# The first tile of a decoder block: x loaded first, its modulation shared by VectorE and TensorE, four weight buffers, and attention's casts queued behind the last hT

## The chip, the cores and the metric

The kernel runs on one core of a Trainium2 chip. The metric is the device time of one execution in microseconds; the time quoted for a kernel is the median of its runs. Engines are called PE (TensorE, with PEld for its weight loads), DVE (VectorE), ACT (ScalarE), POOL (GpSimd) and SP (SyncE, which issues most of the DMAs).

## The reference, cut to what matters

One decoder layer over 512 positions of width 1024, all in float32. The change touches its first stage only: the modulated RMSNorm and the first 768 columns of the input projection.

```python
cs = jax.nn.silu(c)
mod = cs @ w_ada[l] + b_ada[l]
shift1, scale1, gate1, shift2, scale2, gate2 = [m[:, None, :] for m in jnp.split(mod, 6, axis=-1)]
h = _rmsnorm(x, norm1_g[l]) * (1.0 + scale1) + shift1
proj = h @ w_in[l]
qa, ka, va, qd, kd, vd, ga, gd = jnp.split(proj, points, axis=-1)
# sliding-window attention (qa, ka, va), differential attention (qd, kd, vd), gates (ga, gd),
# merge and output projection, then a second modulated RMSNorm, an MLP with a causal convolution, a last RMSNorm
```

shift1 and scale1 are matrix-vector products: each needs 1024 x 1024 weights of w_ada, 4 MB, and they scale and shift h per column.

## The kernel before, in words

Width 1024 is cut into eight tiles of 128 columns (KT = 8), the positions into four tiles of 128 rows (NT = 4). The first stage produces, for each of the eight tiles k, hT(k): 128 columns of h transposed, 128 x 512, as a high part hTh (in fp32r, a rounded float32) and a low part hTl (the rest). A projection tile is then three products: high weights by hTh, low weights by hTh, high weights by hTl. mm_k(k, part) issues one of these for the six banks acc6, which are 768 columns of qa, ka, va: six matmuls of 128 x 128 by 128 x 512 (L334), 18 per tile k. They add up in the same six banks over all eight tiles, so attention can start only after tile 7.

What tile k needs:

- **x**: four transfers of 512 KB into xn (L214). stat(t) squares and sums on ACT (L351), rstd_start does ms on DVE (L171) and a power on POOL (L175), rstd_end finishes on DVE (L181, L185). normalise(t) scales the first HEAD = 256 columns on DVE (L358); scale_x scales the rest on ACT (L381). turn(t) (L363) transposes tile 0, h_turn(k) (L315) the others.
- **The modulation of its 128 columns**: adaw(k), two transfers of 512 KB (scale and shift columns of w_ada; L207) into two buffers. ac_ops forms the sum of the eight weight rows times cs (silu of c) on DVE: two scalings (L256), six multiply-adds (L258), one add (L260), each over 256 columns. reduce_mod sums the 128 partitions on PE with a column of ones (pa, L267), and finish_mod adds bias and gain on DVE (mod, L276, L279). PE issues each float32 matmul as two instructions.
- **hT**: h_tile (L320) writes hTh and hf on ACT from the transposed x with scale and bias from mod; h_low (L324) forms hTl on DVE.
- **Its weights**: w0(k), 384 KB into four raw buffers (L220); split_hi casts them on ACT (L299, L300), split_lo forms the low parts on DVE (L306, L308).

SP issues the transfers in the written order: crow8 (c itself), adaw0, x, w0_0, adaw1, w0_1, and so on. Within a manual schedule DVE, ACT and PE issue in the written order; POOL is outside of it here, and the framework's scheduler placed POOL's constants (qsc, dsw, ddf) and the clearing of va (L436) at the start. keep_warm issues small matmuls into a bank that is not in use yet (L341): 14 at the start, and three behind each of the first three turns.

The loop over the tiles puts the next tile's preparation among the present tile's matmuls: DVE does ac_ops for tile k+1, with h_low(k) in between; PE does the next turn, parts 0 and 1, then the sums pa for tile k+1, then part 2.

Behind the stage comes attention. fill(n) issues n steps of units: a load of eight 128 x 128 weight blocks (L477), a cast on ACT and a low part on DVE (split_pair, L115, L116), and the matmuls (pq, pk, pw; L119 to L121). Each step has three matmuls of 512 columns. evac_q and evac move the six banks out (L430 to L434, L445). ACT and DVE are placed by the scheduler there.

## Time and profile before

| what | value |
|---|---|
| median of 3 runs | 715.82 us (714.96 to 717.16) |
| the profiled execution, its own time | 716.59 us |
| its span, first to last instruction | 714.5 us |
| instructions | 11275 |
| DVE, ACT, POOL busy | 588.5, 384.2, 84.4 us |
| moved by DMA | 121.82 MB, 170 GB/s on the mean |
| DMA, 0 to 20 us and 20 to 62 us | 310 and 254 GB/s |
| first projection matmul of tiles 0, 1, 7 | 19.40, 24.87, 56.44 us |
| first matmul of attention's units (pq) | 60.72 us |

A row of the timeline gives the start and the duration in us, the engine, the line in the kernel, the operation, output and inputs by the program's names, the shapes and a count of merged instructions; in brackets stands the idle time of that engine before it and what ended it. A row of the windows view gives a stretch, its length, the busy time of PE, PEld, DVE, ACT and POOL with the instructions in brackets, the granted TensorE clock as a share of full speed, the mean busy share of the DMA engines and the rate. Times in the trace are from the start of the span. The profiled execution is one of the program's executions; its time differs from the median.

### The profile page before, as it was taken

The page shows a single profiled execution, that of the slowest core. Times are in us where ns is not written, and L with a number is a line of the kernel's source. Part 1 is how long each engine was busy: PE and PEld are TensorE (multiplying, and loading weights), DVE is VectorE, ACT ScalarE, POOL GpSimd, SP SyncE. Part 2 cuts the span into 40 slices and gives each one's busy share as a digit, 9 for nine tenths or more (in the row PEclk, how much of TensorE's full clock was granted, in tenths as well). Part 3 has the DMA queues.
Part 4 walks back from the last instruction along what each step waited for, and adds up shares of the span by engine and source line. Part 5 has one row for each costly group of instructions (what it writes and reads, how often), then busy time and mean ns, then how long its engine had stood idle before and what let it go on. Part 6 is the DMA issues. An engine that isn't in the chain of part 4 may idle for free. (4 is left out here: it accounts for less than half of the span.)

```text
span 714.5 us, 11275 instructions
## 1 busy us (share of the span) xinstructions
PE 688.4 (96%) x4187; PEld 603.0 (84%) x4187; DVE 588.5 (82%) x1125; ACT 384.2 (54%) x677; POOL 84.4 (12%) x101
## 2 busy tenths in 40 slices
PE   5999899999999999999999999999999999999994
PEld 5777778777787888888879999999999999888884
DVE  5998978797986774865479899888889899979996
ACT  3646566455554233432258666555555666656664
POOL 4000000001000100000012021111111102540300
PEclk9999999999999999999999999999999999999998
DMA  9983522453553664737717598877789738996903
GB/s 307 293 264 96 173 64 83 148 163 102 151 159 105 225 196 140 235 118 210 232 59 148 153 201 203 191 185 217 190 199 229 164 123 233 182 203 194 160 0 119
DMA packets 115863, 121.82 MB, mean 170 GB/s; under 512 B 4415, under 2 KB 93280, under 8 KB 115808
## 3 DMA queue, kind: packets, MB, share of 16 engines
q1 hardware_dynamic: 96894, 95.09, 42.1%
q0 software_dynamic: 18720, 25.73, 21.2%
q8 instruction: 33, 0.54, 0.3%
q10 hardware_dynamic: 194, 0.28, 0.1%
q14 instruction: 22, 0.18, 0.1%
HBM read 118.97 MB, written 2.11 MB: 169 GB/s over the span
## 5 line engine op out<-in xcount | busy, mean ns | idle before, releaser
L1133 PE MATMUL up<-t,m_whi 128*128 128x256 f32 x528 | 96.1, 283 | 0.0
L1133 PEld LDWEIGHTS up<-t,m_whi 128*128 128x128 f32 x528 | 82.3, 192 | 0.0
L1133 PE MATMUL up<-t,m_wlo 128*128 128x256 f32 x264 | 74.7, 283 | 0.1
L1133 PE MATMUL up<-bh,p_wlo 128*128 128x256 f32 x232 | 65.7, 284 | 0.6 <-DVE p_wlo L1076 0.6
L1133 PE MATMUL up<-bh,p_whi 128*128 128x256 f32 x232 | 65.6, 283 | 0.0
L1133 PE MATMUL up<-bl,p_whi 128*128 128x256 f32 x232 | 65.6, 283 | 0.0
L1133 PEld LDWEIGHTS up<-t,m_wlo 128*128 128x128 f32 x264 | 50.6, 192 | 0.3 <-DVE m_wlo L1076 0.3
L1133 PEld LDWEIGHTS up<-bh,p_wlo 128*128 128x128 f32 x232 | 44.4, 192 | 1.1 <-DVE p_wlo L1076 1.1
L1133 PEld LDWEIGHTS up<-bh,p_whi 128*128 128x128 f32 x232 | 44.5, 192 | 0.0
L1133 PEld LDWEIGHTS up<-bl,p_whi 128*128 128x128 f32 x232 | 44.5, 192 | 0.0
L1044 POOL DMA_DIRECT2D s<-in_w_up_dram x21 | 27.2, 1385 | 143.0 <-DMA s<-in_w_up_dram 92.7
L764 DVE SCALAR_TENSOR_TENSOR arow<-ra,cs,arow 128x512 f32<-128x512 f32 x56 | 41.9, 748 | 1.4 <-DMA ra<-in_w_ada_dram 0.7
L1076 DVE TENSOR_TENSOR m_wlo<-s,m_whi 128x1024 fp32r<-128x1024 f32 x31 | 37.7, 1216 | 2.0 <-ACT m_whi L1072 2.0
L1072 ACT CAST m_whi<-s 128x1024 fp32r<-128x1024 f32 x31 | 32.5, 1047 | 9.3 <-DVE s L1066 5.9
L1133 PE MATMUL up<-t,p_whi 128*128 128x256 f32 x176 | 32.2, 283 | 0.0
L175 POOL TENSOR_TENSOR r<-ms,mhalf 128x1 f32<-128x1 f32 (+1 forms) x16 | 13.4, 838 | 144.7 <-DVE ms L173 77.2
L694 ACT ACTIVATE sd<-sd,dmx 128x128 f32<-128x128 f32 (+3 forms) x32 | 17.8, 556 | 22.0 <-DVE dmx L692 15.4
L777 POOL DMA_DIRECT2D mod_rows<-arow x8 | 4.3, 540 | 200.5 <-ACT arow L776 200.3
L1133 PEld LDWEIGHTS up<-t,p_whi 128*128 128x128 f32 x176 | 27.4, 192 | 0.2 <-issue 0.2
L1140 ACT ACTIVATE gT<-a,cv 128x512 f32<-128x512 f32 x22 | 17.7, 813 | 17.6 <-DVE a L1175 17.3
L1072 ACT CAST p_whi<-wa 128x1024 fp32r<-128x1024 f32 x18 | 18.7, 1042 | 12.0 <-PE up L1133 10.8
L1133 PE MATMUL up<-t,p_wlo 128*128 128x256 f32 x88 | 24.9, 283 | 0.0
(485 smaller groups left out, 2119.5 us busy)
## 6 DMA issues: line engine op xcount, KB each, us to landing
ra<-in_w_ada_dram SPq DMA_DIRECT2D x32, 512.0 KB, 4.2
wa<-in_w_up_dram SPq DMA_DIRECT2D x22, 512.0 KB, 4.6
s<-in_w_up_dram SPq DMA_DIRECT2D x21, 512.0 KB, 5.0
s<-in_w_up_dram POOLq DMA_DIRECT2D x21, 512.0 KB, 6.5
adaw<-in_w_ada_dram SPq DMA_DIRECT2D x16, 512.0 KB, 5.1
w<-in_w_in_dram SPq DMA_DIRECT2D x12, 512.0 KB, 3.9
a<-in_w_up_dram SPq DMA_DIRECT2D x11, 512.0 KB, 4.7
b<-in_w_down_dram SPq DMA_DIRECT2D x10, 512.0 KB, 3.9
```

The costliest lines, as they stand in the source:

```text
L175: nc.gpsimd.tensor_tensor(r0, ms, mhalf[:, :n], ALU.pow)
L694: nc.scalar.activation(pm[m], pm[m], AF.Exp, bias=mx[:, m : m + 1], scale=slope, accum_out=lsum[:, m : m + 1])
L764: nc.vector.scalar_tensor_tensor(ac, r[:, a], cc, ac, ALU.mult, ALU.add)
L777: nc.gpsimd.dma_start(mod_rows[idx : idx + 1, hf * S : (hf + 1) * S], row)
L1044: nc.gpsimd.dma_start(dst, upblock(*blk), accum_op=ALU.add)
L1072: nc.scalar.copy(W[J, name][0], R[J, SRC[name]])
L1076: nc.vector.tensor_sub(lo, R[J, SRC[name]], hi.bitcast(F32))
L1133: nc.tensor.matmul(o[u], w[:, k, cu], b[:, k], start=name in ("p1", "m5", "p2") and k == 0 and x == 0, stop=k == 3 and x == 2, skip_group_ ...
L1140: nc.scalar.activation(grow(j), av[J][:, u], AF.Identity, bias=cv[:, 66 + j : 67 + j], scale=cv[:, 44 + j : 45 + j])
```

## The change

- SP issues x first; crow8 goes to ACT's queue. adaw0 follows in five parts, the scale columns ahead of the shift columns, then w0_0 in two. adaw has four buffers; tiles 1 and 2 load their adaw in four parts.
- Tile 0's modulation: DVE sums three of the eight weight rows (own_rows, once for scale and once for shift, over 128 columns), PE multiplies the other five by cs directly (mod_mm, with the weights stationary and 48 equal columns of cs moving) and adds DVE's sum (own_sum). For tile 1 PE takes three of the eight rows (direct); tiles 2 to 7 leave all eight to DVE. The sums for tiles 1 to 7 have 48 columns in place of one.
- Bias and gain of mod go to ACT (finish_one); hT(0) and the casts of w0_0 are shared by ACT and DVE; tile 0's matmuls take the banks in the order 4, 5, 0, 1, 2, 3.
- normalise(t) and turn(t) follow stat(t) directly; the keep-warm matmuls are 4, 11, 4 and 5. h_turn(1) comes ahead of tile 0's matmuls.
- POOL joins the manual schedule, and its constants and the clearing of va are written behind the loop.
- Attention's first casts on ACT are ordered behind hf(7), by issue_after, which orders the issue of instructions of the same engine only.

```diff
-    nc.sync.dma_start(crow8, c.rearrange("o (a p) -> (o a) p", p=P))
+    nc.scalar.dma_start(crow8, c.rearrange("o (a p) -> (o a) p", p=P))
...
-        aw = pp.tile([P, 2, KT, m * P], F32, tag="adaw", bufs=2, name=f"adaw{k}")
...
-    load_ada(groups[0])
     for t in range(NT):
-        nc.sync.dma_start(xn[:, t], xd[t * P : (t + 1) * P, :])
...
+        load_x(t)
+    for lo in (0, 4):
+        load_ada_part(adaw[0], 0, 0, 1, lo, lo + 4)
+    for lo, hi in ((0, 4), (4, 6), (6, 8)):
+        load_ada_part(adaw[0], 1, 0, 1, lo, hi)
+    load_w0(0, (512, 768))
+    load_w0(0, (0, 512))
+    for g in groups[1:]:
+        load_ada(g, (0, 4, 8) if g[0] < 3 else (0, 8))
+        load_w0(g[0])
...
-    man.enter_context(tc.manual_schedule(engines={nc.vector.engine, nc.scalar.engine, nc.tensor.engine}))
+    man.enter_context(tc.manual_schedule(engines={nc.vector.engine, nc.scalar.engine, nc.tensor.engine, nc.gpsimd.engine}))
+    keep_warm(4)
...
+    def direct(gi):
+        return {1: 3}.get(gi, 0)
+    NB = 48
+    def mod_mm(o, aw, j, lo, hi, start, stop=True):
         for kk in range(lo, hi):
+            nc.tensor.matmul(
+                o, aw[:, j, kk], cs[:, kk : kk + 1].to_broadcast([P, NB]),
+                start=start and kk == lo, stop=stop and kk == KT - 1,
             )
+    def reduce_one(o, gi, j):
+        more = direct(gi)
+        mod_mm(o, adaw[gi], j, KT - more, KT, True, False)
+        nc.tensor.matmul(o, ac[gi][0][:, j], ones[:, 0:NB], start=not more, stop=True)
+    def finish_one(k, o, j):
...
+        if j == 0:
+            nc.scalar.activation(m[:, 0:1], o[:, 0:1], AF.Identity, bias=cb[:, k : k + 1], scale=n1g[:, k : k + 1])
+        else:
+            nc.scalar.activation(m[:, 1:2], o[:, 0:1], AF.Identity, bias=bsh[:, k : k + 1])
...
+    OWN = 3
+    def own_rows(j):
+        for kk in range(OWN):
+            if kk == 0:
+                nc.vector.tensor_scalar_mul(a0[:, j], adaw[0][:, j, kk], cs[:, kk : kk + 1])
+            else:
+                nc.vector.scalar_tensor_tensor(a0[:, j], adaw[0][:, j, kk], cs[:, kk : kk + 1], a0[:, j], ALU.mult, ALU.add)
+    def own_sum(j):
+        nc.tensor.matmul(po[j], a0[:, j], ones[:, 0:NB], start=False, stop=True)
+    keep_warm(11)
...
+    stat(0)
+    normalise(0)
+    turn(0)
+    keep_warm(4)
+    stat(1)
...
+    normalise(1)
+    turn(1)
+    keep_warm(5)
+    stat(2)
+    normalise(2)
+    turn(2)
+    stat(3)
+    own_rows(0)
+    mod_mm(po[0], adaw[0], 0, OWN, 8, True, False)
+    own_sum(0)
+    scale_x(0)
+    scale_x(1)
+    normalise(3)
+    mod_mm(po[1], adaw[0], 1, OWN, 4, True, False)
+    turn(3)
+    own_rows(1)
+    mod_mm(po[1], adaw[0], 1, 4, 8, False, False)
+    own_sum(1)
...
+    nc.scalar.copy(wts[0][0][:, 512:768], w0[0][:, 512:768])
+    finish_one(0, po[0], 0)
+    nc.vector.tensor_copy(wq, rq)
+    nc.vector.tensor_add(m[:, 1:2], po[1][:, 0:1], bsh[:, 0:1])
+    nc.scalar.activation(hTh[0][:, :256], pts[0][:, :256], AF.Identity, bias=m[:, 1:2], scale=m[:, 0:1])
+    nc.vector.tensor_scalar(hTh[0][:, 256:], pts[0][:, 256:], m[:, 0:1], m[:, 1:2], ALU.mult, ALU.add)
+    nc.scalar.activation(hfs[0], pts[0], AF.Identity, bias=m[:, 1:2], scale=m[:, 0:1])
+    split_lo(0, 1)
     split_lo(0, 0)
+    scale_x(2)
+    scale_x(3)
+    h_turn(1)
...
-            ac_ops(gi + 1, 0, AC_CUT)
+            ac_ops(gi + 1, 0, AC_CUT if gi else 2)
         h_low(g[0])
         if nxt:
-            ac_ops(gi + 1, AC_CUT, KT)
+            ac_ops(gi + 1, AC_CUT if gi else 2, KT)
...
+    # behind the loop now: qsc, dsw and ddf on POOL, unchanged
+    va = big.tile([P, 2, 4, 2 * P], F32R, tag="kvB", name="va")
+    nc.gpsimd.memset(va.bitcast(F32), 0.0)
...
-    fill(SWA_FILL[0])
+    with tc.issue_after(tiles[KT - 1].ins):
+        fill(SWA_FILL[0])
```

## The prediction

> **What bounds the kernel now.** I read the page first. Its first part has PE busy for 688.4 of 714.5 us, and the second part puts the thin places at the two ends and near 366 us.

> ```profile
> PE 688.4 (96%) x4187; PEld 603.0 (84%) x4187; DVE 588.5 (82%) x1125; ACT 384.2 (54%) x677; POOL 84.4 (12%) x101
> ...
> PE   5999899999999999999999999999999999999994
> ```

> Of the 26 us in which PE does nothing, 8.9 lie before 20 us (by the windows view PE is busy for 11.11 of the first 20), and much of that busy time is keep-warm work. From 20 to 366 us PE stands for about 6. So whatever brings tile 0's first projection matmul forward should move everything behind it, as long as no other engine takes over. The PE timeline shows that start: start, duration, engine, line, operation, count, and in brackets the idle time before with its releaser.

> ```profile
> 12.62 0.33 PE L363 MATMUL xt<-ident,xn 128*128 128x128 f32 x1 [2.75 <-DVE xn L358]
> 12.79 0.83 PE L341 MATMUL a<-ones,ident 128*128 128x128 f32 x6
> ...
> 16.87 1.49 PE L341 MATMUL a<-ones,ident 128*128 128x128 f32 x6
> 18.15 0.38 PE L363 MATMUL xt<-ident,xn 128*128 128x128 f32 x1
> 18.36 0.61 PE L315 MATMUL xt<-ident,xn 128*128 128x128 f32 x4
> 19.40 1.66 PE L334 MATMUL a<-hThA,w0h 128*128 128x512 f32 x6 [0.43 <-ACT hThA L320]
> ```

> The first projection matmul starts at 19.40. Its chain backwards: ACT's hT(0), x's last transpose, a keep-warm burst queued in front of that transpose, x normalised by DVE (16.44 to 16.79), its statistics on ACT from 13.05, and x itself, which comes behind 1.05 MB of adaw0:

> ```profile
> 9.24 1.06 ACT L351 ACTIVATE sq<-xn 128x1024 f32<-128x1024 f32 x1 [6.39 <-DMA xn<-in_x_dram]
> ```

> Then the windows view, cut at the first matmul of tiles 0, 1, 2, 3 (the columns are PE, PEld, DVE, ACT, POOL, the granted clock, the DMA share and GB/s).

> ```profile
> 19.40:24.87 5.47, 5.31 (x26) 4.25 (x26) 4.94 (x15) 5.47 (x9) 0.00 (x0) 1.00 0.79 263
> 24.87:29.95 5.08, 5.08 (x26) 4.25 (x27) 4.73 (x14) 2.71 (x5) 0.00 (x0) 1.00 1.02 327
> 29.95:35.27 5.32, 5.27 (x30) 4.14 (x28) 5.13 (x15) 2.25 (x5) 0.00 (x0) 1.00 0.87 272
> ```

> A tile takes 5.08 us where PE is alone in deciding (tile 1) and 5.3 to 5.4 in tiles 2 to 5, where DVE is busy for 5.13 to 5.26: DVE finishes ac late, PE's pa matmuls wait (PE starts them 0.2 us after its sixth matmul could have ended), and DVE then waits 0.16 for pa. Last, two rows that price a clash:

> ```profile
> 5.33 1.18 DVE L243 TENSOR_SCALAR cols<-cols 128x8 f32<-128x8 f32 x1
> ...
> 4.69 1.80 POOL L436 MEMSET va<- 128x2048 f32 x1
> ```

> An instruction of the size of L171's (0.15 us) ends at 6.51, right after POOL's memset (6.49). L235 does the same behind POOL's iota (2.91 to 3.46): it ends at 3.48.

> **Step 1, x first.** Today x0 lands 6.97 us after its issue at 2.27. adaw0's 1.05 MB, 3.0 us at the 341 to 366 GB/s of 4 to 7 us, are no longer ahead, and SP starts with x at 0.74 instead of crow8 (0.45 us). So x0 lands at 9.24 - 3.45 = 5.8 at the latest. The other end: adaw0's 1.05 MB were in use 5.55 us after their issue; half of it is 1.5 less, so 0.74 + 4.05 = 4.8. I take 5.25. Three more x tiles, 1.57 MB at 0.40 MB/us (8 to 12 us: 393 to 418 GB/s), are in at 9.1. adaw0 and w0_0, 1.44 MB at 0.35, follow until 13.2; w0_0 in today's order (issued 5.03, 8.9 to landing) gives 13.9 - 0.45 = 13.5. Splitting adaw0 into five issues of 0.37 to 0.5 us keeps SP at under 6 us of issues, so issue is not the limit. crow8 now heads ACT's queue and delays the rows by 0.4 us; their reader (cols) has until 9 us.

> **Step 2, normalisation.** Per x tile: ACT 1.25 (1.06 + 0.19), then DVE ms 0.15, POOL pow 0.65, DVE rt, rst and xn 0.8. In DVE's new order each tile's three steps stand behind the one before, so tiles follow at 1.65. First: 5.25 + 1.25 + 1.65 = 8.15; then 9.8, 11.45; the fourth waits besides for own_rows(0), three instructions on 128 columns (0.75, between nothing and the 1.35 that three on 256 columns take): x is normalised at 13.1. Today: 16.79.

> **Step 3, modulation of tile 0.** Eight whole-width ac instructions and an add on DVE become six half-width ones; the rest is 10 matmuls with 48 columns, two PE instructions each. Nearest rows: 128 columns at full clock, six in 0.67 us (12.79 to 13.46), 0.11 each; one column, 0.09 each. After turn(3) (13.3) eight instructions of shift rows take 0.9, own_sum and its drain 0.4, the add on DVE 0.15. hT(0) is halved between ACT and DVE (0.78 for the whole, so 0.45 to 0.5). First matmul: 15.4, against 19.40: **-4.0**. If PE runs at half clock the 18 mod and sum instructions cost 0.22 each (the burst at 16.87), 1.0 to 1.6 more on this path; with the early ends of x and own_rows it is 14.4.

> **Step 4, tile 0 itself** (5.47 today). PE: parts 0 and 1 take 2.9, six direct matmuls for tile 1's mod 1.3 (12 at 0.11), the sums 0.4, part 2 1.48, the next turn 0.35: 6.45. DVE after hT(0) (15.2): split_lo 1.0, two ac scalings 0.55, h_low 0.6, three ac steps 1.25, the add 0.4: 19.0, just when PE gets there (15.4 + 2.9 + 0.65). But POOL is now in the written order, so the constants stand behind the fourth pow (12.25): eight memsets 1.1 us, iota and selects 2.1, va's memset 1.8, in all until 17.25. DVE's scalings fall at about 16.15, within the memset, and wait 1.1 as L243 did. PE waits the same in front of its first ac sum. Tile 0 takes 7.55: **+2.1**; without the clash +1.0. The ends are +0.7 (no clash, and 0.09 for each small matmul) and +2.8 (the memset is met at its start).

> **Step 5, tiles 1 to 6** (31.57 from tile 1's first matmul to tile 7's). The mod's two DVE instructions (0.20 from start to start) go to ACT, which is busy for only 2.3 of 5.3 us, and DVE stops waiting for pa (0.16): about 4.95 on DVE, under PE's 5.08. 48 columns for one add at most 0.08. So 5.10 five times and 4.78 for tile 6 (5.07 less its wait of 0.27): 30.28, **-1.3**, between -0.3 and -1.6. ACT's two small instructions (0.2 each) fit into the 0.4 us that hT is early today. Four adaw buffers let SP run ahead (it waits 8.9 us for DVE at L207 today): adaw2 lands at 20.8, needed at 21; from then 1.44 MB per tile take 4.1 to 4.3 us.

> **Step 6, entry to attention.** Casts of the first two weights (L115, 1.04 each) now stand behind hf(7) on ACT: they end 2.6 us after tile 7's first matmul, DVE's low parts (1.21 each) at 2.75 and 4.0, and PE asks at 4.3. So nothing, hidden by tile 7's matmuls; if the five evacuations (4.0 us of ACT) came first, up to 4.2. Only ACT is held: loads stay as they are.

> Sum: -4.0 + 2.1 - 1.3 = **-3.2**. The profiled execution took 716.59 (span 714.5), so 713.4; it lay 0.8 above the median of 715.82, so **712.6**.

> **Rivals.** (a) No clash: the scalings miss POOL's memset. For it: adaw1 may come late enough to push them behind 17.25. Then -4.3: 711.5. (a') The clash comes earlier too: POOL's iota and selects (0.34 to 0.61 each, 13.35 to 15.45) meet own_rows(1) and the copy of w0_0 on DVE (13.1 to 14.6), and one select's wait of 0.6 with a part of a second one puts the first matmul 0.8 later: 713.4. For it: L235 behind the iota; against: only single-input DVE instructions are seen waiting, and the trace has none with two SBUF inputs beside a select. [...] (b) Half clock in tile 0. The windows view has it today after a stretch in which PE was thinly used:

> ```profile
> 12.00:15.00 3.00, 1.34 (x11) 1.26 (x11) 1.44 (x9) 2.85 (x6) 1.18 (x2) 0.99 1.16 351
> 15.00:18.35 3.35, 3.24 (x15) 3.24 (x16) 3.13 (x13) 0.01 (x1) 0.79 (x2) 0.50 1.06 335
> ```

> Afterwards the thin stretch is 6.3 to 9 us, and the keep-warm bursts lie before the matmuls, against it; if it holds over tile 0, 1.1 for the mod and up to 1.7 for seven 512-column matmuls at twice 0.235: 712.6 + 1.5 to 2.8, 714.1 at best. [...] (c) Casts behind evacuations at the entry: 4.2 - 3.2, 716.8; half of it, 714.7. Against: the casts are ready 1.5 us before the first evacuation. (d) The other side, slower: transfers set the pace. By adaw7, 11.1 MB have to follow x. At 0.25 MB/us adaw7 lands at 53.7; ac, pa, mod and hT add 4.8, so tile 7 starts at 58.5 instead of 56.44: 717.9. It decides below 0.29. For it: 282 GB/s in 24 to 44 us. Against: that stretch waits for buffers, and 3 to 21 us ran at 359. (e) The reordering does nothing: DVE's serial order (1.65 per x tile against ACT's 1.25) grows until x is normalised as late as today, 16.8, and the time stays near 715; the steps as priced leave 3.7 us to that, which speaks against it.

> **How the numbers follow.** A measurement can tell about 0.3% (2.15 us) from no change. Chances: forecast 0.40 (its ends 711 to 714.9, so 0.34 faster and 0.06 same), (a) 0.20 (faster), (a') 0.10 (half faster, half same), (b) 0.12 (0.03 faster, 0.09 same), (c) 0.08 (0.02 faster, 0.05 same, 0.01 slower), (d) 0.06 (slower), (e) and whatever else falls out in attention's unwritten order 0.04 (0.02 faster, 0.01 same, 0.01 slower). Faster 0.66, same 0.26, slower 0.08. Best ends together: first matmul at 14.4, no clash, tiles -1.4: 710.4; a little below that for attention's order, 709.8. Above, up to the middle of (c): 716.0.

> **What the profile will show.** Right: ACT's first square near 5.3; x's last transpose near 13.2; first 512-column matmul at 15.4; tile 1's at 23, tile 7's at 53.2; DVE's first ac scaling of tile 1 ending with POOL's memset; tiles 2 to 5 at 5.1 with PE unbroken. Wrong: the first square after 6.5, granted clock 0.50 between 15 and 19, PE waiting for DMA in tiles 1 to 3, or an idle PE at the first pq matmul.

## The result, and the profile after

The change makes the kernel a little slower, by 0.34%: 718.61 us median (20 runs, 715.83 to 724.48) against 716.12 (20 runs), a ratio of 1.0034, 95% interval 1.0018 to 1.0051. Forecast were 712.6, and 709.8 to 716.0 as its range. The profiled execution took 717.3 us, its span is 715.1. The first part of its page:

```profile
PE 693.6 (97%) x4221; PEld 607.2 (85%) x4221; DVE 585.4 (82%) x1107; ACT 388.0 (54%) x691; POOL 84.3 (12%) x101
```

PE is busy for 5.2 us more than before, and has 34 more matmul records (4221 for 4187); each comes with a weight load, so these are 68 more PE instructions. PE's timeline at the first matmul of tiles 0 and 7 and at the waits between:

```profile
15.21 1.66 PE L347 MATMUL a<-hThA,w0hi 128*128 128x512 f32 x6 [1.03 <-DVE hThA L431]
...
19.71 0.42 PE L284 MATMUL pa<-ones,ac 128*128 128x48 f32 x2 [0.86 <-DVE ac L263]
...
31.18 0.62 PE L284 MATMUL pa<-ones,ac 128*128 128x48 f32 x4 [0.41 <-DVE ac L263]
...
47.72 0.62 PE L284 MATMUL pa<-ones,ac 128*128 128x48 f32 x4 [1.13 <-DVE ac L263]
...
54.77 1.66 PE L347 MATMUL a<-hThB,w0h 128*128 128x512 f32 x6
```

The windows view, cut at the first matmul of tiles 0, 1, 2 and of tiles 5 and 6 (columns as in the prediction):

```profile
15.21:22.68 7.47, 6.60 (x38) 5.65 (x39) 7.44 (x18) 4.92 (x9) 1.80 (x2) 1.00 1.12 319
22.68:27.75 5.07, 5.07 (x29) 4.22 (x28) 3.62 (x10) 2.88 (x7) 0.00 (x0) 1.00 1.13 311
27.75:33.45 5.70, 5.29 (x30) 4.15 (x28) 5.67 (x15) 2.77 (x7) 0.00 (x0) 1.00 1.14 309
43.56:49.99 6.43, 5.30 (x29) 4.15 (x28) 4.77 (x13) 2.77 (x7) 0.00 (x0) 1.00 0.97 250
```

The start came as forecast: tile 0 at 15.21 (15.4), tile 0 itself 7.47 (7.55), tile 1 at 22.68 (22.95), undisturbed tiles 5.03 to 5.08. Tiles 2 and 5 did not: 5.70 and 6.43. DVE's timeline has the reason, and in its first row the clash with POOL's memset of va (15.19 to 17.01): two scalings take 1.37 in place of 0.61.

```profile
16.05 1.37 DVE L259 TENSOR_SCALAR ac<-adaw,cs 128x256 f32<-128x256 f32 x2
...
26.98 0.61 DVE L259 TENSOR_SCALAR ac<-adaw,cs 128x256 f32<-128x256 f32 x2 [1.41 <-DMA adaw<-in_w_ada_dram]
...
46.95 0.29 DVE L531 TENSOR_TENSOR lp<-lamv 128x128 f32<-128x128 f32 x1 [1.66 <-DMA lamv<-in_diff_lambda_dram]
```

DVE waits for adaw3, and for lambda, which SP now issues at 41.97 (38.83 before) behind loads that keep the queues full: from 8 to 44 us DMA moves 312 GB/s at a share of 1.14 (before 304 at 0.94). Attention's first pq still starts earlier, 59.44 for 60.72. But the span is 0.6 us longer: PE's lead is lost behind the stage, and from 67 us on the instructions of PE, DVE, ACT and POOL stand in the order that they had. Two places in the PE timeline show losses that the kernel before has not, or has less of, in its profile. One is a half clock behind PE's wait of 2.1 us at 71.5 (windows view), 1.65 us:

```profile
70.88:74.29 3.41, 1.31 (x10) 1.01 (x9) 3.41 (x16) 1.78 (x4) 0.00 (x0) 1.00 0.70 215
74.29:77.70 3.41, 3.41 (x13) 2.68 (x11) 2.53 (x4) 0.70 (x2) 0.00 (x0) 0.50 0.03 8
```

The other are two waits of PE for DVE (before: none at pss, 0.24 at td):

```profile
189.31 1.02 PE L797 MATMUL pss<-ones,sq 128*128 128x1 f32 x8 [0.25 <-DVE qkv L497]
198.76 0.63 PE L774 MATMUL td<-ident,sd 128*128 128x128 f32 x4 [0.38 <-DVE sd L765]
```

### The profile page after: what moved, and what is told of

It reads as the page before. It is cut to its first block, busy times and chain, and to the rows that moved or that the text cites. A ratio compares the mean times of both kernels' runs of the same rounds, so it can differ in the third digit from the quotient of the medians.

```text
span 715.1 us, 11342 instructions
## 1 busy us (share of the span) xinstructions
PE 693.6 (97%) x4221; PEld 607.2 (85%) x4221; DVE 585.4 (82%) x1107; ACT 388.0 (54%) x691; POOL 84.3 (12%) x101
## 5 line engine op out<-in xcount | busy, mean ns | idle before, releaser
L160 POOL TENSOR_TENSOR r<-ms,mhalf 128x1 f32<-128x1 f32 (+1 forms) x16 | 12.9, 809 | 144.9 <-DVE ms L158 76.1
```

What stands on the lines that cost most here:

```text
L160: nc.gpsimd.tensor_tensor(r0, ms, mhalf[:, :n], ALU.pow)
```

## The experiments

Each time is a median beside runs of the kernel before on the same chip (714.97 to 715.62). The same kernel run a second time came out 0.0006 (the change) and 0.0014 (lamv_fill) apart in its ratio, so 0.5 to 1 us between two kernels is at the edge.

**Transfers, clash or clock.** First the change once more, and three single edits:

```diff
 half_bytes: -            for j in range(2):      # in load_ada; DVE uses the scale half for shift too
             +            for j in range(1 if k > 1 else 2):
 lamv_early: +        if g[0] == 4:               # sink and lamv issued here, ahead of adaw4
 pool_early: the constants and the memset of va back to the start of the kernel
```

> The changed kernel, unaltered, beside the kernel before. Two theories for the time that is missing behind a start that came 4.2 us earlier. T (transfers): the queue is full from 3 to 44 us at about 310 GB/s, a tile's 1.44 MB take 4.65 us against 5.08 us of matmuls, so any hiccup makes DVE wait for a buffer; the profile will again show DVE waiting on adaw or lamv for 2 us or more in tiles 2 to 6, in other places than in the first profile, and times 1 to 6 us above the best. C (clock): the half-clock window falls at another place in attention because all is shifted; the profile shows 3.4 us at 0.50 somewhere between 60 and 240 us and no DVE wait beyond 1 us. Both: 717 to 719 us median, 0.2 to 0.5% above before.

> For tiles 2 to 7 only the scale half of adaw is loaded, and DVE uses it for the shift as well: 3.1 MB fewer in the stage, the same instructions on every compute engine. The output is not the reference's. T: the waits on adaw3 and lamv go (3.1 us of DVE in the first profile, 1.5 to 2 of it on PE), tile 7 starts at 53.2 or before, the runs lie closer together, and the median falls by 2 to 4 us below the changed kernel's, to 714.5 to 716.5 or lower. C: the median stays at 717.5 to 719.

> The small loads of sink and lamv are issued ahead of adaw4, where they stood behind w0_7. T: DVE's wait of 1.66 us for lamv in front of tile 7's ac sum is gone, PE's wait of 1.13 us there too; tile 7 starts about 1.3 us earlier than in the first profile (53.5), and the median falls by 1 to 1.5 us. C: tile 7 may start earlier, but the median stays.

> POOL's constants and the clearing of va stand at the start again, as before. The clash theory of the prediction: DVE's two ac scalings of tile 1 take 0.6 us instead of 1.37, PE's wait of 0.86 us in tile 0 goes, tile 1 starts 0.8 us earlier (21.9). By T, this is given back at adaw3, where DVE then waits 2.2 instead of 1.4 us, and the median moves by 0 to -0.4. If T is wrong and the start sets the end, -0.8.

Measured: the change 718.12, ratio 1.0040 [1.0024, 1.0057]; half_bytes 716.37, 1.0011 [0.9996, 1.0026]; lamv_early 716.64, 1.0030 [1.0016, 1.0045]; pool_early 718.29, 1.0037 [1.0021, 1.0053]. Transfers are a part: without DVE's waits for DMA, half_bytes has all of tiles 1 to 5 at 5.03 to 5.08, and its ratio is 0.0023 to 0.0029 (1.6 to 2.1 us) below the change's. The clash is none that shows in the time: in pool_early DVE's two scalings take 0.61 and PE's wait of 0.86 is gone, but half clock fell into tile 0 of that profile (7.98) and the median is that of the change. And something else is left, since half_bytes moves 3 MB less and is still not faster than before. The mean granted clock of all runs is the same, 0.9938 before and after, so a clock that fell more often is not the difference: one more stretch of 3.41 us at half clock in every execution would lower it by 0.0024.

**Where attention gives the lead back.** DVE's timeline near 178 us, in the change:

```profile
181.50 0.49 DVE L827 TENSOR_SCALAR arow<-ra,cs 128x512 f32<-128x512 f32 x1 [2.05 <-DMA mod_rows<-arow]
```

arow has one buffer. Its row is written out (mod_rows, 2 KB, issued by POOL), and DVE can start the next arow only when that write has landed. In the profile before DVE waits 0.35 there, in the five profiles of the change and its edits 1.67 to 2.21. DVE has hardly a gap in the next 15 us, so the delay passes on to PE as the waits of 0.25 and 0.38 above. The DMA packets show why. Among those of the change's profile are 33 code loads: single packets of 16,384 bytes on a queue of the kind instruction (q8), which take 0.89 to 1.38 us. All through the kernel 202 to 300 PE records (matmuls and weight loads, 253 on the mean) lie between two of them, while the instructions of DVE there vary from 19 to 75 and those of ACT from 14 to 53, so they are taken as PE's. The change puts 68 more instructions ahead of attention, so later loads come some 4 to 6 us earlier: the one at 183.3 comes at 176.9 to 179.4 in these five. In the change's profile 30 of the write's 32 packets start between 179.19 and 179.37, the code load runs from 179.44 to 180.43, and the last two packets start at 180.41 and 180.43, when it ends. That is 1.0 of the 1.7 us by which the write lands later; the landing itself then follows 1.0 us behind the last packet instead of 0.4, for a reason that the trace does not give. Three runs on this; the edits are

```diff
 before_pad: +    pad(8)                            # 17 one-column matmuls where PE is idle
             +    pad(9)
 lamv_phase: -            nc.tensor.matmul(acc6[5][:, :P], ones, ones, ...)      # 24 of them
             +            nc.tensor.matmul(acc6[5], ones, ones[:, 0:1].to_broadcast([P, S]), ...)   # 6
```

> The kernel before once more, unchanged, for a second profile of it. Three theories of why attention gives back the lead of the changed kernel. L (code loads): the changed kernel has 34 more matmul records ahead of attention, so every later 16,384-byte code load of the PE queue falls some 6 us earlier; the one at 177.1 to 179.4 us then stands on a DMA engine between the pieces of the small mod_rows write (issued by POOL at about 176 to 178), the write lands 1.0 to 1.3 us later, and DVE, which needs its buffer (arow), waits 1.7 to 2.2 us instead of 0.35. A (attention's pace): DVE and the loads have a time of their own there, and whatever lead PE brings is waited away. N (noise of the start): the profiled execution of before had a half clock ahead of its first projection matmul, so an ordinary execution starts about 1 us earlier, and the lead was never 2 us. Expected here: L and A: DVE's wait for mod_rows near 178 is again 0.2 to 0.6 and the code load again at 182 to 184. N: the first 512-column matmul at 18.3 to 18.6 instead of 19.40, and the first sw matmul at about 61.2 instead of 62.20. Time 715 to 716 by all.

> The kernel before, with 17 one-column fp32 matmuls (34 records, 68 PE instructions) in two stretches at its start in which PE is idle (2.6 to 4.8 and 9.9 to 12.6 us). Nothing else of its order changes. L: the code load that fell at 183.3 falls at 176 to 179, DVE's wait for mod_rows grows from 0.35 to 1.5 to 2.2 us, PE loses 0.4 to 1.0 us near 188, and the whole is 0.5 to 2 us slower than before (716.0 to 717.5, if no other load is met or missed). A and N: the wait stays at 0.2 to 0.6 and the time within 0.4 us of before.

> The changed kernel with sink and lambda loaded ahead of adaw4 (the run in which that alone was done gave 716.64), and its 24 keep-warm matmuls of 128 columns replaced by 6 of 512 columns: 36 records, 72 PE instructions, fewer, so that PE's code loads fall where they fell in the kernel before. L: code load near 183 less the lead (about 181), DVE's wait for mod_rows at 0.2 to 0.8 instead of 2.21, no PE wait for qkv at the pss matmuls, and 0.7 to 2 us less than 716.64: 714.6 to 716. A: the wait is about 2 us wherever the code loads fall, and the time stays at 716.2 to 717. N: as A. If the wider bursts warm the clock less, half clock shows between 15 and 21 us, as it did in three of the five profiles, and costs up to 0.8.

before_again: 715.39, 1.0002 [0.9989, 1.0015]. Its profile, span 712.6, has the same short wait, with the code load at 182.64:

```profile
178.52 0.49 DVE L762 TENSOR_SCALAR arow<-ra,cs 128x512 f32<-128x512 f32 x1 [0.28 <-DMA mod_rows<-arow]
```

before_pad: 718.52, 1.0046 [1.0029, 1.0063]. The load falls at 182.34, the write is issued at 181.06, and DVE waits as in the change:

```profile
184.35 0.49 DVE L768 TENSOR_SCALAR arow<-ra,cs 128x512 f32<-128x512 f32 x1 [1.91 <-DMA mod_rows<-arow]
```

That is theory L's wait, in the kernel before, from 68 instructions. Of the 3.2 us by which the kernel is slower at most 0.85 belongs to it (PE's loss there in the profile): the pads took 0.1 to 0.2 us a record and put the first matmul 2.2 us later. lamv_phase: 719.31, 1.0053 [1.0037, 1.0069]. The wait is 0.25 as L says, but the time went the other way: with the wide bursts the clock was at half from 14.66 to 21.49 (tile 0 took 8.81; once more at 76.1), and the load, now at 184.36, fell beside the load of wga, for which ACT waited 3.94: it was used 6.8 us after its issue, 4.1 in the change. In the kernel before the same transfer lands after 5.7 and 6.1 us in the two profiles in which the code load falls into it, after 3.5 and 3.7 in before_fill and before_fill_both, where it doesn't. A code load moved out of one transfer's way may stand in that of the next.

**The clock, cheaply.** PE's 2.1 us at 71 filled with 9 matmuls into a bank that is free there, and in the changed kernel 4 ahead of the first projection matmul:

```diff
+            if (i, j, b) == (0, 0, 1):            # in swa_transpose
+                idle = vbank("idle")
+                for _ in range(9):
+                    nc.tensor.matmul(idle[:, :P], ident, ones, start=True, stop=True)
...
     h_turn(1)
+    keep_warm(4)
```

> The changed kernel with sink and lambda loaded ahead of adaw4, and 13 more keep-warm matmuls (26 records, 52 PE instructions) in two places where PE only waits: 4 ahead of the first projection matmul (14.2 to 15.2 us), 9 in the 2.1 us at about 71 us in which PE waits for DVE's pTl. DVE's order moves in a few places (a cast's low part, three arow steps). L (code loads meet transfers): the code load that fell at 177.1 falls about 4.5 us earlier, ahead of the mod_rows write; DVE's wait for that write is 0.2 to 0.8 instead of 2.21, and PE's two waits of 0.40 (pss) and 0.37 (td) at 187 and 196 us shrink to less than half. C (clock): besides, no half clock can follow the filled 2.1 us; in the profiles so far it followed in two of two of the changed kernel, none of lamv_early. Time 715.0 to 716.0 by L and C together, 715.8 to 716.4 by C alone; if neither matters, 716.64 as lamv_early.

> The kernel before with the 9 matmuls in the 2.1 us at about 72 us alone (18 records, 36 PE instructions; a few DVE instructions change places). C: executions that fell to half clock there no longer do, so that the median falls by up to 0.6 us: 714.7 to 715.3. L: its code load moves from 182.6 to about 179.4, just behind the mod_rows write (178.0) if that lands in 1.2 us: the wait stays under 1 us; if they meet, DVE waits 1.5 or more and PE loses up to 0.9: up to 716.2.

lamv_fill: 713.91, 0.9976 [0.9962, 0.9990], faster than the kernel before. before_fill: 713.95, 0.9986 [0.9976, 0.9997]. The fill lies in the wait:

```profile
70.53 2.17 PE L664 MATMUL idle<-ones,ident 128*128 128x128 f32 x18
72.80 0.55 PE L669 MATMUL tp<-ident,st 128*128 128x128 f32 x3
```

In lamv_fill L put DVE's wait for mod_rows at 0.2 to 0.8; it is 1.54. The matmuls at 71 also moved a few DVE instructions in each kernel that has them: PE loses 0.4 at 75 us and gains 0.7 at 90, so 0.3 of a fill's gain is neither clock nor code load. Both parts alone, and the change with both:

> The changed kernel itself (sink and lambda last, as in the change) with both fills of the run before (4 keep-warm matmuls ahead of the first projection matmul, 9 in PE's 2.1 us at 71). C (clock): the fills take away the half-clock stretches of 3.41 us, which cost 0.5 at the start and 1.65 at 74 us, as they did with lambda early (716.64 to 713.91): about 715.4 here, and the difference to lamv_fill, 1.5, is what the transfers cost (T). If the fills only help together with lambda early, 717 or more.

> lambda early, with only the 4 matmuls ahead of the first projection matmul (16 PE instructions). C: half clock at 15 to 21 us in fewer executions, half clock at 74 in as many as ever: 715.8 to 716.4. L (code loads): the code load that fell at 177.1 falls 1.5 us earlier, about 175.7, so that DVE's wait for mod_rows is 1 to 2.2 and the loss at 187 to 196 stays: 716 or more.

> lambda early, with only the 9 matmuls at 71 us. C: no half clock at 74; it may still show at 15 to 21, where it costs 0.5 to 0.8: 714.2 to 715.4, so that this fill has the larger part of the 2.7 us. L: the load falls 3.3 us earlier (about 174), DVE's wait for mod_rows is 0.3 to 1.5. If neither counts, 716.6.

after_fill: 715.27, 0.9997 [0.9983, 1.0012]; lamv_fill_start 715.89, 1.0000 [0.9986, 1.0014]; lamv_fill_mid 714.95, 0.9991 [0.9979, 1.0002]. All lie where C put them, and L's wait came out wrong in lamv_fill_mid (2.29, expected 0.3 to 1.5) and right in lamv_fill_start (1.62). But after_fill's profile has lost the wait for mod_rows too:

```profile
178.37 0.49 DVE L832 TENSOR_SCALAR arow<-ra,cs 128x512 f32<-128x512 f32 x1 [0.27 <-DMA mod_rows<-arow]
```

**Clock against code loads.** The 13 fills are 52 instructions. Three wide ones cover the same time with 12, in the same order on every engine:

```diff
-    keep_warm(4)
+    nc.tensor.matmul(acc6[5], ones, ones[:, 0:1].to_broadcast([P, S]), start=True, stop=True)
...
-                for _ in range(9):
-                    nc.tensor.matmul(idle[:, :P], ident, ones, start=True, stop=True)
+                for _ in range(2):
+                    nc.tensor.matmul(idle, ident, ones[:, 0:1].to_broadcast([P, S]), start=True, stop=True)
...
 before_fill_both: -WARM = 14
                   +WARM = 20
```

> As after_fill, but PE's two idle places are filled with few wide matmuls (1 and 2 of 512 columns, 12 PE instructions) in place of 13 of 128 columns (52): the same order on every engine, nearly the same time of PE busy, but the code loads stay within 1 us of where the change put them. C alone: 715.3, as after_fill. L: the load still stands beside the mod_rows write, DVE waits 1.5 to 2.2 us for it instead of 0.27, and the time is 0.5 to 1.0 above after_fill: 715.8 to 716.3.

> As lamv_fill with the wide matmuls. C alone: 713.9, as lamv_fill. L: DVE's wait for mod_rows 1.5 to 2.2 (in lamv_fill 1.54 of the earlier 2.21), so 0 to 0.8 above lamv_fill: 713.9 to 714.7.

> The kernel before with the 9 matmuls at 72 us and 6 more in its keep-warm burst (until about 11 us, where PE then waits for x). If the 19.40 of the profile before was late by half clock (theory C): first projection matmul at 16.9 to 17.2 in an ordinary execution, tile 1's at about 23.0, no half clock at 14 to 18, and 713.2 to 713.9 against the 713.95 with the 9 alone; then the change's earlier start is worth nothing where the clock is undisturbed, since its tile 1 also starts at 22.7 to 23.0. If the late start has another cause, first matmul at 18.5 to 19.5 and 714 as with the 9 alone.

after_fill_wide: 717.12, 1.0032 [1.0020, 1.0044], against 0.9997 with the narrow fill; the mean clock of the runs is 0.9956 and 0.9960. So the clock has about 0.3 us (0.0004 of 715) of the difference of 0.0035, 2.5 us, which the two intervals leave uncertain by about 0.002; and against the unfilled change (1.0034, 1.0040) the wide fill, clock cover with few instructions, brought only 0.1 to 0.6 us. Up to 165 us the two profiles agree within 0.05 us; then

```profile
180.37 0.49 DVE L832 TENSOR_SCALAR arow<-ra,cs 128x512 f32<-128x512 f32 x1 [2.01 <-DMA mod_rows<-arow]
```

and PE loses 1.2 us by 208, and 1.5 more at 367, where ACT and DVE wait for a load of wa. L had expected 715.8 to 716.3, so the time rose by more than this wait explains. The DMA view of 177 to 180 us in that profile (queue, kind, packets, MB, share; the last column of the issue is the time from issue to landing):

```profile
q1 hardware_dynamic: 133, 0.24, 20.8%
q8 instruction: 1, 0.02, 2.3%
q0 software_dynamic: 32, 0.00, 0.7%
...
mod_rows<-arow POOLq DMA_DIRECT2D x1, 2.0 KB, 3.4
```

One code load, and the write lands 3.4 us after its issue. The same view of after_fill, 176.6 to 179:

```profile
q1 hardware_dynamic: 148, 0.27, 29.2%
q0 software_dynamic: 32, 0.00, 0.8%
...
mod_rows<-arow POOLq DMA_DIRECT2D x1, 2.0 KB, 1.6
```

No code load, 1.6 us. lamv_fill_wide: 715.14, 1.0004 [0.9994, 1.0015], a wait of 1.79 and a time above the 713.9 to 714.7 of L; the clock cover brought 1.9 us here (from 1.0030), and L has 1.0 to 2.0 between this and the narrow fill (0.9990 in its repeat below, 0.9976). before_fill_both: 716.29, 1.0019 [1.0010, 1.0028], expected 713.2 to 713.9: first matmul at 17.02, tile 1 at 23.07, as expected where no half clock falls, but its code load falls at 178.43 and the wait is 2.36. The edit is not clean either: the scheduler moved transfers and DVE instructions too, so that DVE's low part of attention's first weights (L116, 1.22) stands in front of the ac sum of tile 7, for which PE waits 1.13 at 53. So it is slower, with a clock of 0.996.

The attention instructions of PE are the same in all kernels, so a profile's loss there can be read as the shift of PE's starts against before_again, from 155-168 to 203-215 us. With the wait at 0.35 or less it is 0.00 to 0.38 in six profiles (both of before, before_fill, after_fill, and the two that follow); with 1.54 to 2.36 it is 0.53 to 1.57 in twelve. lamv_phase alone, with the load of wga, breaks the rule (0.25, and 1.35).

The write itself has no exception in the 19 profiles. In the twelve in which a code load starts or runs while the write is in flight, 30 of its 32 packets start within 0.2 us, the last two when the load ends, and it lands 2.9 to 3.7 us after its issue. In the seven without one all 32 start within 0.25 us and it lands after 1.6 to 1.7. That a code load in flight delays this write, and DVE with it, is shown; how much of a kernel's median it makes is not.

The same shift gives the account of the change's first profile against before_again: 0.5 ahead at 62 us, 1.2 behind at 80 (the half clock at 74), 2.3 behind at 205, 1.8 at 350 and 2.4 at the end.

Last, the load moved a little further by a third fill, 4 matmuls into pa where PE waits for ac of tile 1:

> The version with lambda early and both fills once more (713.91 before), to be compared on one chip with the next: 713.5 to 714.3.

> As lamv_fill, with a third fill: 4 small matmuls of 48 columns (8 records, 16 PE instructions) where PE waits for DVE's ac of tile 1 (19.4 us, 0.63 to 0.9 us idle). L: the code load that stood at 176.1 beside the mod_rows write moves some 1.5 us further ahead, DVE's wait falls from 1.54 to 0.3 to 0.8 and the time by 0.2 to 0.6 to 713.3 to 713.7. C: the clock was undisturbed already, so 713.9 as before. If the third fill delays the ac sum, up to 0.3 more.

lamv_fill_again: 714.65, 0.9990 [0.9977, 1.0003]; lamv_fill3: 713.66, 0.9979 [0.9968, 0.9990], the lowest median, with the ratio of lamv_fill's first run (0.9976). The repeat lies above the 713.5 to 714.3 that was expected. The wait of lamv_fill3 is 0.27, below L's 0.3 to 0.8, but so it is in lamv_fill_again, which is lamv_fill unchanged (1.54 there): the load fell at 176.13 in one execution and at 173.27 in the other. Loads move by up to 3 us between executions, so that a collision is more or less likely and seldom certain (this is one pair; two profiles each of before and of the change differ by 0.6 and 0.7), and this last pair doesn't tell L from the fill itself.

## Why the prediction was wrong, step by step

**Steps 1 to 3 held in their times, in part by luck, and not in their worth.** The first square came at 4.59 (5.25), the first matmul at 15.21 (15.4). Two misses cancelled there: x's last transpose came at 12.34 (13.2), and hT(0), which was to be halved into 0.45 to 0.5, took 1.13 where the whole had taken 0.78, since DVE's half waits for ACT's:

```profile
14.02 0.56 ACT L430 ACTIVATE hThA<-xt,mod 128x256 fp32r<-128x256 f32 x1 [0.92 <-DVE mod L429]
14.61 0.54 DVE L431 TENSOR_SCALAR hThA<-xt,mod 128x256 fp32r<-128x256 f32 x1 [0.69 <-ACT hThA L430]
```

But the -4.0 was set against 19.40, and that was no property of the kernel. The stretch 15.00 to 18.35 at 0.50, which the prediction quoted as a rival's mark, lay on the very chain to 19.40. In before_again PE's rows still have it:

```profile
14.66 1.49 PE L341 MATMUL a<-ones,ident 128*128 128x128 f32 x6
...
18.68 0.50 PE L334 MATMUL a<-hThA,w0h 128*128 128x512 f32 x1 [0.43 <-ACT hThA L320]
```

In before_fill, whose start is unaltered, the clock is whole and the burst takes 0.83:

```profile
14.18 0.83 PE L341 MATMUL a<-ones,ident 128*128 128x128 f32 x6
...
16.96 1.43 PE L334 MATMUL a<-hThA,w0h 128*128 128x512 f32 x5 [0.43 <-ACT hThA L320]
```

There tile 1 starts at 23.01, in before_fill_both at 23.07; in the ten profiles of the changed start without half clock at 22.68 to 23.39. So steps 3 and 4 together, -4.0 + 2.1 = -1.9, are worth about nothing once the clock is the same: before, too, tile 0 takes 6.05 when it starts at 16.96. This is the first failed step: the sum's largest term took as its base an execution with half clock on the path. In the change's own two profiles half clock falls behind PE's wait at 72 us instead (1.6 each), where before's two have none. In time, too, lamv_fill (0.9976, 0.9990 in its repeat) and before_fill (0.9986) are not told apart. The 0.8 that was taken off because the execution lay above the median is of the same kind: against before_again it is 0.7 late at 62 us and loses 1.5 more at 367.

**Step 4** was right: the clash is there, two scalings of 0.30 each took 1.37 beside the memset, and tile 0 took 7.47. Rival (a') didn't show.

**Step 5** is the second failed step, and was mis-sized: -1.3 against 32.09 in the place of 31.57, +0.5. Its DVE and PE prices hold (5.03 to 5.08). What failed is "needed at 21; from then 1.44 MB per tile take 4.1 to 4.3": at the 0.31 MB/us that a full queue gave, adaw3 came 1.41 late, and lambda, which the prediction never followed past the loads, 1.66. That was rival (d) at a smaller scale. Tiles 1 to 6 took 30.76 to 32.09 in five profiles with lambda late, and 30.55 to 31.94 in the eight with lambda early, in seven of which DVE still waits 0.8 to 1.4 for an adaw. The prediction also forgot that pcv's transpose, within tile 6 before, now stands behind tile 7: +0.4. The price of the late lambda is 0.5 to 1.5 us by after_fill against lamv_fill's repeat and lamv_fill, and 0.3 to 0.7 by the change against lamv_early; these intervals overlap, so it is an estimate.

**Step 6** held: pq did not wait for the casts.

**The rule behind the sum** failed too: "whatever brings tile 0's first projection matmul forward should move everything behind it", as long as no other engine takes over. PE's own code loads broke it: the 34 added records move all of them (1.1 to 11.1 us earlier in the change's profile than in before's), and at 177 to 180 us one met the mod_rows write. Moving the loads is worth 2.5 us by the pair after_fill and after_fill_wide, 1.0 to 2.0 by lamv_fill, its repeat and lamv_fill_wide. With the late lambda (0.3 to 1.5) this makes an estimate of 1.3 to 4; measured are 2.4 to 2.9 against the kernel before. That the change has the loads' collision in both of its own profiles and in each of its three first edits (2.05, 1.67; 2.04, 2.21, 1.92) is shown; that the whole of the 2.5 comes through this one write isn't. By the profiles it is 0.5 to 1.6 of PE's time, and 1.5 of the pair's difference arose at 367. Seven profiles of both kernels lose 0.6 to 2.1 there (before's first 1.5); in these the load of s issued near 350 lands after 6.1 to 7.5 us, in the other twelve after 4.6 to 5.7. They have no common mark in the code loads, and why this load is slow stays open. Rival (b), half clock in tile 0, came in after_again (tile 0 took 7.97), half_bytes and pool_early; on the mean the clock is no difference.

## What to carry to other kernels

Before a wait in a profile is counted as a gain, look whether the granted clock was whole on the chain that leads to it; an execution's lottery is no term of a sum. An added instruction can cost more than its time: here 68 of them moved PE's code loads, and a 2 KB write that one buffer waits for met one, so a change of under 1% should be judged with its instruction count changed too. Matmuls in PE's wait of 2.1 us brought 1.0 us in the kernel before. In the changed kernel, with the few ahead of the first projection matmul, they brought 0.1 to 1.9 as three wide ones and 2.6 to 3.9 as thirteen narrow ones, which moved the code loads as well; where the clock was whole, the reordering of the start brought tile 1 forward by -0.4 to 0.3.
